# High and low part of each weight tile, 32 bytes apart modulo 64, under the 256-column passes of a two-layer encoder

## The chip, the cores and the metric

The kernel runs on one core of a Trainium2 chip, with no communication. The metric is the device time of one execution in microseconds (us). A profiled execution gives the time of every instruction on TensorE (PE, and PEld for its weight loads), VectorE (DVE), ScalarE (ACT), GpSimd (POOL) and SyncE (SP), and of the transfers.

## The reference

Two layers over 512 positions of 1024 channels, float32. Each layer has a half-step FFN, a mixer of three branches and a second half-step FFN, all behind an RMSNorm and a shift, scale and gate worked out from `c`:

```python
def swiglu(h, w_gate, w_up, w_down):
    return (jax.nn.silu(h @ w_gate) * (h @ w_up)) @ w_down
...
    for l in range(DEPTH):
        mod = (c_act @ w_ada[l] + b_ada[l]).reshape(B, N_MOD, D_MODEL)
        h = modulate(rms_norm(x, norm_gain[l, 0]), mod[:, 0], mod[:, 1])
        x = x + 0.5 * mod[:, 2][:, None, :] * swiglu(h, ffn_w_gate[l, 0], ffn_w_up[l, 0], ffn_w_down[l, 0])
        h = modulate(rms_norm(x, norm_gain[l, 1]), mod[:, 3], mod[:, 4])
        x = x + mod[:, 5][:, None, :] * hybrid_mixer(h, w_in[l], ...)
        h = modulate(rms_norm(x, norm_gain[l, 2]), mod[:, 6], mod[:, 7])
        x = x + 0.5 * mod[:, 8][:, None, :] * swiglu(h, ffn_w_gate[l, 1], ffn_w_up[l, 1], ffn_w_down[l, 1])
```

An FFN has 2816 hidden channels. The mixer (attention in chunks, trailing averages, attention with forget gates, their gated sum and an output map) has no part in the change but for its weight tiles' slots.

## The kernel before, in words

**Precision.** Every float32 operand is split into a high part, rounded to float32r, and the low remainder. ScalarE casts the high part (`nc.scalar.copy`), VectorE subtracts (`lo = raw - hi`). A product is three matmul passes, high·high, high·low, low·high, in that order: `triple` (lines 119 to 121) or, in the seven-product scheme, `add_product` (lines 128 to 130). In the order of the weight operand that is high, high, low, then the next 128 channels' high, high, low. A pass streams 512 columns of the moving operand, or 256.

**The FFN.** Hidden tiles of 128 channels are made in three parts of 6, 8 and 8. Some are made directly, with 512-column passes (`Ffn.unit`): all six of the first part in the opening FFN, the first four in the other three FFNs. The rest come in pairs from `seven`, which makes a product of a 2x2 block matrix with seven block products instead of eight. It loads two weight tiles, forms the sums S1 to S4 on VectorE, splits everything, and runs seven block products of four `add_product` steps each, all of 256 columns: A11·B11, A12·B21, S2·T2, S1·T1, S3·T3, S4·B22, A22·T4. `seven` is called for the gate and then for the up weights of a pair, by turns. The right-hand blocks T1 to T4 and B lie in `b`, `hhi` and `hlo`. The down projection runs in `k_outer`, weights outermost, 512 columns a pass. The last half of an FFN's down projection, and of the mixer's output map, is split into two halves of 256 columns (`before_last` given); there `prefetch_weights` also fetches the next stage's first weight tiles.

**Tiles.** `st(shape, dtype, tag, bufs)` takes a slot of a tag. High parts of weights have the tag `whi`, low parts `wlo`, three slots each of 4096 bytes a partition; in `seven`, A11/A12 and A22 are there, and the split sums S1/S2 and S3/S4 are in two tiles of tag `ptb` (two slots of 8192 bytes), high half first. Prefetched weights (`spare`) lie in `ptb` or `b`. `raw` receives the transfers, issued on SyncE's queue. Tags are laid out in order of first use and each slot's size is rounded up to 32 bytes. `whi`, `wlo`, `v2` and the tags ahead of them start on multiples of 64 bytes; `nt_v4` has 16 bytes, so `raw`, `t1`, `t2` and `ptb`, which follow it, start at 32 past a multiple of 64.

**Order.** The tile framework sets the order of instructions on each engine from the order of the program and its priorities, and semaphores where tiles are shared. Work on the side (the modulation's dot products on VectorE, norms) is spread by `later` and `poll`, which count passes by `pe[0]`.

Of the kernel before, what the change touches and what calls it, by code (L numbers as in the profile page):

```python
# [15 lines left out]
F32 = mybir.dt.float32  # L16
F32R = mybir.dt.float32r
# [5 lines left out]
P = 128  # L23
T = 512
D = 1024
KD = D // P
# [3 lines left out]
H = 8  # L30
# [10 lines left out]
def encoder_kernel(tc, xT, c, w_ada, b_ada, gains, w_gate, w_up, w_down, w_qkv, w_f, w_ubg,  # L41
# [18 lines left out]
    def nm(s):  # L60
        uid[0] += 1
        return f"{s}_{uid[0]}"

    def st(shape, dt, tag, bufs):
        return sb.tile(shape, dt, tag=tag, bufs=bufs, name=nm(tag))

    def acc(shape=(P, T)):
        return ps.tile(list(shape), F32, tag="acc", bufs=4, name=nm("acc"))

    def mmt(shape=(P, T)):  # L70
        return ps.tile(list(shape), F32, tag="mm", bufs=4, name=nm("mm"))

    def blk(tag, dt=F32R):
        bufs = {"xv": 4, "v2": 4, "b": NB}[tag]
        return st([P, 2, T], dt, tag, bufs)
# [65 lines left out]
    nc.scalar.dma_start(crow, c)  # L141
    nc.scalar.activation(crow, crow, AF.Silu)
    x_blocks, squares, crows = [], [], []
    for b in range(4):
        xb = blk("xv", F32)
        nc.sync.dma_start(xb, xT[:, 2 * b:2 * b + 2, :])
        x_blocks.append(xb)
        sq = st([P, 2, T], F32, "wlo" if b else "whi", 3)
        for a in range(2):
            nc.scalar.activation(sq[:, a, :], xb[:, a, :], AF.Square)  # L150
        squares.append(sq)
        if b < 2:
            pc = mmt()
            mm(pc, ones[0:1, :], crow[:, b * T:(b + 1) * T], start=True, stop=True)
            crows.append(pc)
# [117 lines left out]
                mod_credit[0] -= 1.0  # L273
                mod_pop()

    def wchunk(src, shape, side=True, spare=None, lo_eng=None):
        lo_eng = lo_eng or nc.vector
        side_work(side)
        raw = st([P] + list(shape), F32, *(("b", NB) if spare else ("raw", NRAW)))
        last["dma"] = nc.sync.dma_start(raw, src).ins  # L280
        if spare == "ptb":
            both = st([P, 2] + list(shape), F32R, "ptb", 2)
            hi, lo = both[:, 0], both[:, 1]
        elif spare == "b":
            hi = st([P] + list(shape), F32R, "b", NB)
            lo = st([P] + list(shape), F32R, "b", NB)
        else:
            hi = st([P] + list(shape), F32R, "whi", 3)
            lo = st([P] + list(shape), F32R, "wlo", 3)
        with behind("scalar"):  # L290
            nc.scalar.copy(hi, raw)  # L291
        with behind("vector"):
            lo_eng.tensor_tensor(lo, raw, hi.bitcast(F32), op=ALU.subtract)  # L293
        return hi, lo
# [102 lines left out]
    def split_to(hi, lo, src):  # L397
        nc.scalar.copy(hi, src)  # L398
        nc.vector.tensor_tensor(lo, src, hi.bitcast(F32), op=ALU.subtract)  # L399


    def k_outer(chunk_src, nch, lhs_rhs, before_last=None):

        if before_last is None:
            parts, nheld = [(None, slice(0, T), [acc() for _ in range(4)])], 2
        else:
            parts = [(hs, slice(hs * HALF, (hs + 1) * HALF), [b((P, HALF)) for _ in range(4)])
                     for hs, b in enumerate((mmt, acc))]  # L410
            nheld = 3

        def go(part, j, chunks):
            _, cols, accs = part
            for c, hi, lo in chunks:
                for kk in range(2):
                    a, b, x, y = lhs_rhs(hi[:, kk, :], lo[:, kk, :], 2 * c + kk, j)
                    triple(accs[j], a, b, x[:, cols], y[:, cols], start=(c == 0 and kk == 0),
                           stop=(c == nch - 1 and kk == 1))

        held = []
        for c in range(nch):
            if before_last is not None:
                if c == nch - 2:
                    quiet[0] = 8
                    before_last()
                quiet[0] = 8
            hi, lo = wchunk(chunk_src(c), (2, T))
            if c < nch - nheld:
                for part in parts:  # L430
                    for j in range(4):
                        go(part, j, [(c, hi, lo)])
            else:
                held.append((c, hi, lo))
        if before_last is not None:
            quiet[0] = 5
        for part in parts:
            for j in range(4):
                go(part, j, held[:-2])
            for j in range(4):  # L440
                go(part, j, held[-2:])
                yield j, part[0], part[2][j]
# [23 lines left out]
    def minus(o, a, b):  # L466
        nc.vector.tensor_tensor(o, a, b, op=ALU.subtract)  # L467
# [51 lines left out]
            q0, cols = {"T1": (0, FIRST), "T3": (0, SECOND), "T4": (2, FIRST), "T2": (2, SECOND)}[name]  # L519
            return [tuple(part[:, k % 2, cols] for part in self.parts[q0 + k // 2]) for k in range(4)]  # L520

    def seven(srcs, blocks, bank):

        raws = []
        for src in srcs:
            side_work()
            raw = st([P, KD, P], F32, "raw", NRAW)
            last["dma"] = nc.sync.dma_start(raw, src).ins
            raws.append(raw)
        tens = lambda o, a, b, op: nc.vector.tensor_tensor(o, a, b, op=op)  # L530
        a11, a12, a21, a22 = raws[0][:, :4], raws[0][:, 4:], raws[1][:, :4], raws[1][:, 4:]
        ah, al = st([P, KD, P], F32R, "whi", 3), st([P, KD, P], F32R, "wlo", 3)
        split_to(ah, al, raws[0])
        bh, bl = st([P, 4, P], F32R, "whi", 3), st([P, 4, P], F32R, "wlo", 3)
        split_to(bh, bl, a22)
        s12, s34 = st([P, 2, 4, P], F32, "v2", 4), st([P, 2, 4, P], F32, "v2", 4)
        tens(s12[:, 0], a21, a22, ALU.add)
        minus(s34[:, 0], a11, a21)
        minus(s12[:, 1], s12[:, 0], a11)
        minus(s34[:, 1], a12, s12[:, 1])  # L540
        pair12, pair34 = st([P, 2, 2, 4, P], F32R, "ptb", 2), st([P, 2, 2, 4, P], F32R, "ptb", 2)
        split_to(pair12[:, 0], pair12[:, 1], s12)
        split_to(pair34[:, 0], pair34[:, 1], s34)
        lefts = {"A11": [(ah[:, k], al[:, k]) for k in range(4)],
                 "A12": [(ah[:, 4 + k], al[:, 4 + k]) for k in range(4)],
                 "A22": [(bh[:, k], bl[:, k]) for k in range(4)]}
        for name, pair, i in (("S1", pair12, 0), ("S2", pair12, 1), ("S3", pair34, 0), ("S4", pair34, 1)):
            lefts[name] = [(pair[:, 0, i, k], pair[:, 1, i, k]) for k in range(4)]
        x, y, w = bank((P, HALF)), bank((P, HALF)), bank((P, HALF))
        c = st([P, 4, HALF], F32, "v2", 4)  # L550
        go = lambda o, left, right, start: add_product(o, lefts[left], blocks.operand(right), start)
        go(x, "A11", "B11", True)
        nc.scalar.copy(c[:, 0], x)
        go(y, "A12", "B21", True)
        tens(c[:, 0], y, c[:, 0], ALU.add)
        go(x, "S2", "T2", False)
        nc.scalar.copy(c[:, 1], x)
        go(w, "S1", "T1", True)
        nc.scalar.copy(c[:, 2], w)
        go(x, "S3", "T3", False)  # L560
        nc.scalar.copy(c[:, 3], x)
        go(w, "S4", "B22", False)
        tens(c[:, 1], w, c[:, 1], ALU.add)
        tens(c[:, 3], c[:, 2], c[:, 3], ALU.add)
        go(x, "A22", "T4", False)
        return [[c[:, 0:2].rearrange("p a t -> p (a t)")], [x, c[:, 3]]]
# [10 lines left out]
    class Ffn:  # L577
# [9 lines left out]
            self.norm = Norm(self.l, self.ms, xtag)  # L587

        def prefetch_weights(self):
            self.pre = [self.gate_up(0, 0, spare="ptb"), self.gate_up(1, 0, spare="ptb"), self.gate_up(0, 1, spare="b")]  # L590

        def unit(self, o, w, cols=slice(0, T), ks=range(KD)):
            for k in ks:
# [16 lines left out]
        def run(self, nxt):  # L610
            l, s, ms = self.l, self.s, self.ms
            in_ffn[0] = True
            mod_tag[0] = "v2"
            parts = ((0, 6), (6, 8), (14, 8))
            for part, (f0, nf) in enumerate(parts):
                acts = []
                n = 0
                if part == 0 and self.norm is None:
                    acts = self.start()
                    n = 3  # L620
                    blocks = Blocks()
                elif part == 0:
# [17 lines left out]
                    n = 2  # L640
                    blocks = Blocks(self.norm.xa, modc[:, l, 3 * ms])
# [16 lines left out]
                    blocks.finish()  # L658
                while n < nf:
                    both = [apply(p, AF.Silu)  # L660
                            for p in seven([w_gate[l, s, f0 + n + i] for i in range(2)], blocks, acc)]
                    ups = seven([w_up[l, s, f0 + n + i] for i in range(2)], blocks, mmt)
                    for i, sg in enumerate(both):
                        acts.append(self.act(n + i, None, ups[i], sg))
                    n += 2
# [235 lines left out]


    def forget(l):
        raw = st([P, KD, H], F32, "wf", 1)
        nc.sync.dma_start(raw, w_f[l])
        f2 = st([P, KD, 40], F32R, "ssum", 1)
        nc.gpsimd.memset(f2.bitcast(F32), 0.0)
# [10 lines left out]
        a = t2(T)[:H, :]  # L918
# [9 lines left out]
        for i in range(NT):  # L928
            n = (i + 1) * P
# [383 lines left out]
```

## Time and profile before

| | |
|---|---|
| median of 3 runs | 2387.72 us (2385.93 to 2392.21) |
| the profiled execution | 2390.61 us, its span 2388.7 us |
| TensorE busy | 2352.5 us, 98% of the span, 14322 matmuls |
| VectorE busy | 1766.9 us, 74% |
| ScalarE busy | 1219.5 us, 51% |
| transfers | 320.95 MB, mean 134 GB/s |

A matmul's record in the profile runs from its start to its modelled end and overlaps the next one's; how long a pass holds the engine is the spacing of two starts. Line numbers are those of the kernel before. A group's row gives the engine, the operation, the tiles written and read (`acc<-b,whi`: into `acc`, moving operand `b`, weights `whi`), shape and count.

### The profile page before, as it was taken

What the parts mean: (1) busy time and instruction counts of PE and PEld (TensorE: products, weight loads), DVE (VectorE), ACT (ScalarE), POOL (GpSimd) and SP (SyncE); (2) the same over time, 40 slices, a digit from 0 to 9 for tenths busy, and PEclk for the clock granted to TensorE, in tenths of its full rate; (3) what the DMA queues carried; (4) which work ended last, traced back from release to release, by engine and by line L of the source; (5) the groups of instructions that cost most, each with busy time, mean ns of one, the idle gap of its engine ahead of it and who ended that gap; (6) DMA issues with size and microseconds to landing.
All of it is one profiled execution on the core that took longest, in us unless ns stands there. A gap on an engine that the chain in (4) does not pass through costs nothing.

```text
span 2388.7 us, 37374 instructions
## 1 busy us (share of the span) xinstructions
PE 2352.5 (98%) x14322; PEld 2093.0 (88%) x14322; DVE 1766.9 (74%) x3147; ACT 1219.5 (51%) x2129; POOL 314.8 (13%) x401
## 2 busy tenths in 40 slices
PE   7999999999999999999999999999999999999999
PEld 5898998778888898989999989888788888999898
DVE  8887866787685577878687878677876855878583
ACT  5353555786632353535553536466865324636262
POOL 3000011144412200000100000112443122000000
PEclk9999999999999999999999999999999999999999
DMA  8535342323355524353415353523233654143323
GB/s 278 192 106 185 99 167 80 94 76 112 113 198 207 185 72 159 115 183 101 150 63 177 99 184 107 185 72 115 73 114 110 220 197 173 62 141 107 98 101 103
DMA packets 116438, 320.95 MB, mean 134 GB/s; under 512 B 11138, under 2 KB 13314, under 8 KB 116260
## 3 DMA queue, kind: packets, MB, share of 16 engines
q1 hardware_dynamic: 115106, 314.38, 39.7%
q0 software_dynamic: 1152, 4.19, 0.4%
q8 instruction: 112, 1.84, 0.3%
q14 instruction: 66, 0.54, 0.1%
q10 hardware_dynamic: 2, 0.00, 0.0%
HBM read 312.16 MB, written 6.38 MB: 133 GB/s over the span
## 4 chain that ended last, share of the span: by engine, by line
PE 84%; DVE 7%; ACT 5%; issue 2%; DMA 2%; SPq 0%; ACTq 0%; DVEq 0%
PE acc L119 15%; PE acc L120 15%; PE acc L121 15%; PE acc L128 4%; PE acc L129 4%; PE mm L128 4%; PE mm L129 4%; PE acc L130 4%; PE mm L130 4%; PE mm L119 3%; PE mm L121 3%; PE mm L120 3%; DVE v L206 1%; ACT b L863 1%; PE mm L1001 1%
## 5 line engine op out<-in xcount | busy, mean ns | idle before, releaser
L291 ACT CAST whi<-raw 128x1024 fp32r<-128x1024 f32 (+1 forms) x255 | 264.8, 1043 | 376.5 <-PE acc L120 246.0
L293 DVE TENSOR_TENSOR wlo<-raw,whi 128x1024 fp32r<-128x1024 f32 x247 | 303.8, 1233 | 154.2 <-ACT whi L291 153.0
L119 PE MATMUL acc<-b,whi 128*128 128x512 f32 (+1 forms) x960 | 360.6, 376 | 0.0
L120 PE MATMUL acc<-b,whi 128*128 128x512 f32 (+1 forms) x960 | 357.0, 372 | 0.0
L121 PE MATMUL acc<-b,wlo 128*128 128x512 f32 (+1 forms) x960 | 356.6, 371 | 0.0
L121 PEld LDWEIGHTS acc<-b,wlo 128*128 128x128 f32 x960 | 180.8, 188 | 31.7
L119 PEld LDWEIGHTS acc<-b,whi 128*128 128x128 f32 x960 | 180.8, 188 | 31.2
L120 PEld LDWEIGHTS acc<-b,whi 128*128 128x128 f32 x960 | 181.0, 189 | 29.6
L399 DVE TENSOR_TENSOR ptb<-v,ptb 128x1024 fp32r<-128x1024 f32 x140 | 171.2, 1224 | 36.9 <-ACT ptb L398 36.8
L398 ACT CAST ptb<-v 128x1024 fp32r<-128x1024 f32 x140 | 146.7, 1051 | 100.8 <-DVE v L467 52.7
L119 PE MATMUL acc<-hhi,whi 128*128 128x512 f32 x480 | 191.2, 400 | 3.3 <-ACT hhi L728 1.7
L120 PE MATMUL acc<-hlo,whi 128*128 128x512 f32 x480 | 187.9, 392 | 2.1 <-DVE hlo L731 2.1
L121 PE MATMUL acc<-hhi,wlo 128*128 128x512 f32 x480 | 187.6, 391 | 0.0
L398 ACT CAST whi<-raw 128x1024 fp32r<-128x1024 f32 (+1 forms) x140 | 116.7, 834 | 120.6 <-PE acc L120 55.2
L399 DVE TENSOR_TENSOR wlo<-raw,whi 128x1024 fp32r<-128x1024 f32 (+1 forms) x140 | 133.2, 951 | 8.2 <-ACT whi L398 6.8
L119 PE MATMUL acc<-whi,hhi 128*128 128x512 f32 x336 | 137.8, 411 | 0.9 <-DVE xv L399 0.9
L121 PE MATMUL acc<-whi,hlo 128*128 128x512 f32 x336 | 132.0, 393 | 0.0
L120 PE MATMUL acc<-wlo,hhi 128*128 128x512 f32 x336 | 131.7, 392 | 0.0
L206 DVE CUSTOM_DVE_ANT_0 v<-v,b,badac 128x1024 f32<-128x1024 f32 x87 | 115.7, 1339 | 12.3 <-DMA v<-in_w_ada_dram 12.2
L448 DVE SCALAR_TENSOR_TENSOR xv<-acc,modc,xv 128x512 f32<-128x512 f32 (+1 forms) x112 | 77.1, 691 | 56.3 <-PE acc L121 56.2
L129 PE MATMUL acc<-b,ptb 128*128 128x256 f32 x420 | 118.1, 281 | 0.0
L129 PE MATMUL mm<-b,ptb 128*128 128x256 f32 x420 | 118.1, 281 | 0.0
(313 smaller groups left out, 6662.2 us busy)
## 6 DMA issues: line engine op xcount, KB each, us to landing
raw<-in_w_down_dram SPq DMA_DIRECT2D x88, 512.0 KB, 4.4
v<-in_w_ada_dram SPq DMA_DIRECT2D x87, 512.0 KB, 4.9
raw<-in_w_up_dram SPq DMA_DIRECT2D x82, 512.0 KB, 3.6
raw<-in_w_gate_dram SPq DMA_DIRECT2D x79, 512.0 KB, 3.6
b<-in_w_ada_dram SPq DMA_DIRECT2D x57, 512.0 KB, 5.3
raw<-in_w_ubg_dram SPq DMA_DIRECT2D x56, 512.0 KB, 3.6
raw<-in_w_qkv_dram SPq DMA_DIRECT2D x42, 512.0 KB, 3.8
raw<-in_w_branch_dram SPq DMA_DIRECT2D x24, 512.0 KB, 3.7
```

The source lines that it names most:

```text
L119: mm(o, lh, rh, start=start, stop=False)
L120: mm(o, lh, rl, start=False, stop=False)
L121: mm(o, ll, rh, start=False, stop=stop)
L128: mm(o, lh, rh, start=start and k == 0, stop=False, skip_group_check=True)
L129: mm(o, lh, rl, start=False, stop=False, skip_group_check=True)
L130: mm(o, ll, rh, start=False, stop=k == 3, skip_group_check=True)
L206: dot = nc.vector.tensor_tensor_reduce(out=raw, in0=raw, in1=silc[0], scale=1.0, scalar=badac[:, l, j, d:d + 1], op0=ALU.mult, op1=ALU.add ...
L291: nc.scalar.copy(hi, raw)
L293: lo_eng.tensor_tensor(lo, raw, hi.bitcast(F32), op=ALU.subtract)
L398: nc.scalar.copy(hi, src)
L399: nc.vector.tensor_tensor(lo, src, hi.bitcast(F32), op=ALU.subtract)
L448: nc.vector.scalar_tensor_tensor(x, acc_j, gate, x, op0=ALU.mult, op1=ALU.add)
```

## The change

A new helper, `duo`, takes one slot for both parts of a tile: 4·512+16 words, the high part from the start and the low part from word 1024, each moved by a number of words that a table `PLACES` gives for the tag and the place. `whi` and `wlo` become one tag `w`, and `ptb` weights use `duo` too. For `w`, place 0 moves neither part; place 1 moves the high part 32 bytes and the low part 64; place 2 moves the low part 32 bytes. For `ptb`, place 0 moves both 32 bytes, place 1 the low part 32, place 2 the high part 32 and the low part 64. `seven` takes place 1 for the gate and place 2 for the up weights; the split `k_outer` takes place 1; the prefetched first gate and up tiles take 1 and 2; all else takes 0. The squares of the start lie in two `w` slots, and the forget weights' 256 bytes move from a tag of their own into `yl`.

```diff
+    PLACES = {("w", 0): (0, 0), ("w", 1): (8, 16), ("w", 2): (0, 8),
+              ("ptb", 0): (8, 8), ("ptb", 1): (0, 8), ("ptb", 2): (8, 16)}
+
+    def duo(shape, tag="w", place=0, raw=False):
+
+        t = st([P, 4 * T + 16], F32R, tag, {"w": 3, "ptb": 2}[tag])
+        n = int(np.prod(shape))
+        parts = []
+        for base, at in zip((0, 2 * T), PLACES[tag, place]):
+            v = t[:, base + at:base + at + n]
+            if len(shape) == 2:
+                v = v.rearrange("p (a b) -> p a b", a=shape[0])
+            elif len(shape) == 3:
+                v = v.rearrange("p (a b c) -> p a b c", a=shape[0], b=shape[1])
+            parts.append(v)
+        return parts
...
+    sq_parts = duo((2, T)) + duo((2, T))
...
-        sq = st([P, 2, T], F32, "wlo" if b else "whi", 3)
+        sq = sq_parts[b].bitcast(F32)
...
-    def wchunk(src, shape, side=True, spare=None, lo_eng=None):
+    def wchunk(src, shape, side=True, spare=None, lo_eng=None, place=0):
...
         if spare == "ptb":
-            both = st([P, 2] + list(shape), F32R, "ptb", 2)
-            hi, lo = both[:, 0], both[:, 1]
+            hi, lo = duo(shape, "ptb", place)
...
         else:
-            hi = st([P] + list(shape), F32R, "whi", 3)
-            lo = st([P] + list(shape), F32R, "wlo", 3)
+            hi, lo = duo(shape, "w", place)
...
-            hi, lo = wchunk(chunk_src(c), (2, T))
+            hi, lo = wchunk(chunk_src(c), (2, T), place=0 if before_last is None else 1)
...
-    def seven(srcs, blocks, bank):
+    def seven(srcs, blocks, bank, place):
...
-        ah, al = st([P, KD, P], F32R, "whi", 3), st([P, KD, P], F32R, "wlo", 3)
+        ah, al = duo((KD, P), "w", place)
         split_to(ah, al, raws[0])
-        bh, bl = st([P, 4, P], F32R, "whi", 3), st([P, 4, P], F32R, "wlo", 3)
+        bh, bl = duo((4, P), "w", place)
...
-        pair12, pair34 = st([P, 2, 2, 4, P], F32R, "ptb", 2), st([P, 2, 2, 4, P], F32R, "ptb", 2)
-        split_to(pair12[:, 0], pair12[:, 1], s12)
-        split_to(pair34[:, 0], pair34[:, 1], s34)
+        pair12, pair34 = duo((2, 4, P), "ptb", place), duo((2, 4, P), "ptb", place)
+        split_to(*pair12, s12)
+        split_to(*pair34, s34)
...
-            lefts[name] = [(pair[:, 0, i, k], pair[:, 1, i, k]) for k in range(4)]
+            lefts[name] = [(pair[0][:, i, k], pair[1][:, i, k]) for k in range(4)]
...
-            self.pre = [self.gate_up(0, 0, spare="ptb"), self.gate_up(1, 0, spare="ptb"), self.gate_up(0, 1, spare="b")]
+            self.pre = [self.gate_up(0, 0, spare="ptb", place=1), self.gate_up(1, 0, spare="ptb", place=2), self.gate_up(0, 1, spare="b")]
...
-                            for p in seven([w_gate[l, s, f0 + n + i] for i in range(2)], blocks, acc)]
-                    ups = seven([w_up[l, s, f0 + n + i] for i in range(2)], blocks, mmt)
+                            for p in seven([w_gate[l, s, f0 + n + i] for i in range(2)], blocks, acc, 1)]
+                    ups = seven([w_up[l, s, f0 + n + i] for i in range(2)], blocks, mmt, 2)
...
-        raw = st([P, KD, H], F32, "wf", 1)
+        raw = st([P, KD, H], F32, "yl", 1)
```

## The prediction

> **What bounds the kernel now.** I read the page first: the busy shares, the slices, the chain of waits.
>
> ```profile
> span 2388.7 us, 37374 instructions
> PE 2352.5 (98%) x14322; PEld 2093.0 (88%) x14322; DVE 1766.9 (74%) x3147; ACT 1219.5 (51%) x2129; POOL 314.8 (13%) x401
> ...
> PEclk9999999999999999999999999999999999999999
> ...
> PE 84%; DVE 7%; ACT 5%; issue 2%; DMA 2%; SPq 0%; ACTq 0%; DVEq 0%
> ```
>
> TensorE is busy for 98% of the span at the full granted clock, and the chain that ends last is 84% TensorE. Passes queue without gaps, so what a pass costs is not its record but its spacing: start to start with the next one. The windows view and the timeline give it. First, by stage: a stretch of eight pairs of seven-product calls (`seven`), and one split `k_outer`:
>
> ```profile
> core 0: us, PE busy (x) PEld busy (x) DVE busy (x) ACT busy (x) POOL busy (x), PEclk, DMA share, GB/s
> 954.89:1034.72 79.83, 79.83 (x673) 79.83 (x672) 70.10 (x105) 46.62 (x80) 0.00 (x0) 1.00 0.41 128
> 833.08:849.63 16.55, 16.55 (x139) 16.55 (x138) 10.67 (x12) 9.76 (x16) 4.86 (x5) 1.00 0.31 96
> ```
>
> (673 and 139 count one pass that reaches over an edge.) 79.83 us / 672 is 118.8 ns a pass in `seven`; 16.55 / 138 is 119.9 ns in the split `k_outer`. TensorE has no gap in either, and DVE's 70.10 us leave 12% of the first. All are 256-column passes; they still do not all cost the same. The tile view shows it (minimum/median/maximum of the record, ns):
>
> ```profile
> L128 PE MATMUL mm<-hhi,whi x280: 283/283/283, 134.9 to 2332.9; 128*128 128x256 f32 x140
> L129 PE MATMUL acc<-hlo,ptb x140: 277/280/285, 132.1 to 2328.7; 128*128 128x256 f32 x140
> L130 PE MATMUL acc<-hhi,ptb x140: 274/278/281, 132.3 to 2328.8; 128*128 128x256 f32 x140
> ```
>
> Same shape, same kind of moving operand; only the weight tile differs. With `whi` every record is 283, locked; with `ptb` it drifts from 277 to 285; and line 130 alone has records down to 274.
>
> The code says what differs. Slots are laid out by tag in order of first use. `hhi`, `hlo`, `b`, `xv`, `whi`, `wlo` and `v2` start on multiples of 64 bytes. Then comes the 16-byte `nt_v4` in a place of 32, and `raw`, `t1`, `t2` and `ptb` behind it start 32 past a multiple. So `whi`/`wlo` weights are in class 0, `ptb` weights in class 32, and the moving operands of these rows in class 0. Now the timeline over the two kinds of switch (start us, record us, instruction):
>
> ```profile
> 127.64 0.28 PE L130 MATMUL acc<-hhi,wlo 128*128 128x256 f32 x1
> 127.76 0.28 PE L128 MATMUL acc<-b,ptb 128*128 128x256 f32 x1
> 127.87 0.28 PE L129 MATMUL acc<-b,ptb 128*128 128x256 f32 x1
> 127.99 0.28 PE L130 MATMUL acc<-b,ptb 128*128 128x256 f32 x1
> ...
> 133.20 0.28 PE L129 MATMUL acc<-hlo,ptb 128*128 128x256 f32 x1
> 133.32 0.27 PE L130 MATMUL acc<-hhi,ptb 128*128 128x256 f32 x1
> 133.43 0.28 PE L128 MATMUL acc<-b,whi 128*128 128x256 f32 x1
> 133.55 0.28 PE L129 MATMUL acc<-b,whi 128*128 128x256 f32 x1
> 133.66 0.28 PE L130 MATMUL acc<-b,wlo 128*128 128x256 f32 x1
> ...
> 134.86 0.28 PE L128 MATMUL mm<-hhi,whi 128*128 128x256 f32 x1
> ...
> 137.74 0.28 PE L128 MATMUL mm<-b,ptb 128*128 128x256 f32 x1
> ```
>
> 134.86 to 137.74 is 24 class-0 passes in 2.88 us: 120 ns each, locked. That goes with the record of 283, so record less 163 is about the spacing. 127.76 to 133.43 is 48 class-32 passes in 5.67 us: 118.1 ns. The switch 32 to 0 (pass at 133.32, record 0.27, the 274 above) has about 111 to 113 ns, and the three passes from it take 0.34 us against 0.36 for three locked ones. The switch 0 to 32 (127.64) has 0.12 and then 0.11: three passes in 0.35. Other calls repeat it at the same places:
>
> ```profile
> 143.30 0.27 PE L130 MATMUL mm<-hhi,ptb 128*128 128x256 f32 x1
> 143.41 0.28 PE L128 MATMUL mm<-b,whi 128*128 128x256 f32 x1
> 143.53 0.28 PE L129 MATMUL mm<-b,whi 128*128 128x256 f32 x1
> 143.64 0.28 PE L130 MATMUL mm<-b,wlo 128*128 128x256 f32 x1
> ...
> 153.28 0.27 PE L130 MATMUL acc<-hhi,ptb 128*128 128x256 f32 x1
> ...
> 153.62 0.28 PE L130 MATMUL acc<-b,wlo 128*128 128x256 f32 x1
> ```
>
> 0.34 us both times. Today such switches come twice in 84 passes. The change makes them come twice in three.
>
> **The change, part by part.**
>
> *1. High and low part in opposite classes, in `seven`.* A `w` slot has 4·512+16 words, 8256 bytes or 129·64, so all its slots start in class 0, and those of `ptb` stay in class 32. The places add 0, 32 or 64 bytes. Gate (place 1): high in class 32, low in class 0, in both tags. Up (place 2): high 0, low 32. Each group of three passes uses high, high, low, so it has one pair of equal weights and two switches. A gate group, from the rows: high to low (32 to 0) 113 ns, low to high (0 to 32) 118, and the equal pair behind a switch to 32, which began 127.76, 116 (0.11 to 0.12): 347 ns. An up group: 118, 113, and 117 for the equal pair behind a switch to 0: 348. The mean is 115.8 ns against 118.8 now. `Ffn.run` calls `seven` twice for each pair of hidden tiles: 1, 4 and 4 pairs in three FFNs, 4 and 4 in the opening one, so 3·18 + 16 = 70 calls of 7·4·3 = 84 passes: 5880. They lie on the path (no gap in that window): 5880 · 3.0 ns = 17.6 us less.
>
> No row shows such a mix in steady state, so I bound it: every pass at the shortest record, 274 (about 112.5 ns), saves 5880 · 6.3 ns = 37 us; every pass at the longest, 285 (about 122), costs 5880 · 3.2 = 19 us. I take the switch rows, because they are the same operation, repeated at three places with the same answer.
>
> *2. The split `k_outer`, place 1.* 4 FFNs and 2 output maps, 192 passes each, 1152: from 119.9 to the gate group's 115.7: 4.8 us less. Bounds as before: 8.5 less, 2.4 more.
>
> *3. The prefetched first gate and up tile in `ptb`.* 288 passes (3 FFNs · 2 tiles · 8 · 2 halves · 3). Gate and up alternate here from one k to the next, and opposite order puts low next to an equal high: one switch each way in six passes, not two. I take half the effect, about 1.5 ns: 0.4 us less.
>
> *4. The mixer's two prefetched tiles, default place, now class 0.* They are the moving operand of 96 passes:
>
> ```profile
> 384.65 0.39 PE L119 MATMUL acc<-ptb,hhi 128*128 128x512 f32 x1
> ...
> 385.82 0.39 PE L120 MATMUL acc<-ptb,hhi 128*128 128x512 f32 x1
> ...
> 1057.19 0.39 PE L119 MATMUL acc<-b,whi 128*128 128x512 f32 x1
> ...
> 1058.78 0.39 PE L120 MATMUL acc<-b,whi 128*128 128x512 f32 x1
> ```
>
> Five spacings in 1.17 us are 234 ns; seven in 1.59 are 227. 96 · 7 ns = 0.7 us less. All other 512-column weight tiles stay in class 0 (place 0) and keep 227.
>
> *5. One slot for both parts.* A high tile's slot now comes free with the low part's last pass, one pass (0.23 us) later. The group view has who feels it:
>
> ```profile
> L291 ACT CAST whi<-raw 128x1024 fp32r<-128x1024 f32 (+1 forms) x255 | 264.8, 1043 | 376.5 <-PE acc L120 246.0
> ```
>
> and the waits of TensorE (us in all, times, longest) have what it costs there:
>
> ```profile
> PE acc L119 <- ACT whi L291: 1.6, 2, 0.8
> PE mm L119 <- ACT whi L291: 1.5, 1, 1.5
> ```
>
> The cast waits for that slot often (246.0 us), with DVE's subtraction queued behind it, but TensorE waits for a cast only three times, 3.1 us in all: the other two slots cover it. I cost it at 0.5 us; uncovered at all of ScalarE's 88 such waits it would be 88 · 0.23 = 20 us, which the three waits exclude. The opening squares hold two of three slots until DVE's fold, long before the second weight tile's cast. The small forget weights move into `yl`, idle then; its one transfer on SP's queue waits for nothing.
>
> *Sum:* 17.6 + 4.8 + 0.4 + 0.7 − 0.5 = 23 us. The profiled execution took 2390.6 us (span 2388.7), 0.1% above the median of 2387.7, so the scale is the same: 2388 − 23 is 2365. I put 2366, as DVE, at 70.10 of 79.83 us, would come to 90% of that stage and may hold back a little. The bounds of parts 1 and 2 set the forecast's own range: 2352 (three quarters of the 45 us) to 2378.
>
> [...] The rows above have 283 throughout with one weight tile and 274 to 285 with another. [...]
>
> **The rivals.**
>
> *Paid back.* The short pass at a switch belongs to the state that the long drift before it left; the mix settles near the drifting 118 ns. For: the 12 passes 133.43 to 134.86 take 1.43 us, 119.2 each, so a switch is mostly gone after a few passes. Against: the gain itself is not taken back in them, 1.43 us against 1.44 for twelve locked. At 117.3 ns: 5880 · 1.5 + 1152 · 2.6 = 12 us, 2376; at 118, 2381.
>
> [...]
>
> *Slower: the mix catches at the long spacing.* Class 0 alone locks at 120; alternating classes could lock as well, and at a drift's longest records (285, about 122 ns) rather than its shortest. The place is `seven` and the split `k_outer`; it decides from a mean of 118.8 up; at 122 it costs 19 + 2 = 21 us: 2409; half of it 2398. For: a lock exists, and the drift holds such records. Against: each switch seen so far ran short, none long.
>
> **How the numbers follow.** Forecast 0.55; paid back 0.15; nothing 0.10; slower 0.20. The range reaches from the forecast's low end, 2352, over paid back and nothing to the mildest of slower, 2394. About 0.3% (7 us) is what a measurement of this kernel can tell from no change. Faster: 0.55 and most of paid back, 0.67. Same: the rest of it and nothing, 0.13. Slower: 0.20.
>
> **What would show it.** Right: the stretch of eight pairs of calls takes 77.5 to 78.5 us instead of 79.83, with TensorE still gapless; a 138-pass split takes 16.0; weight records in `seven` leave 283 for about 274 to 281; 512-column spacing stays 227. Paid back: records spread round 280 and the stretch takes 79. Slower: records of 285 as the median. Wrong in part 5: new idle time of TensorE behind casts.

## The result, and the profile after

The changed kernel took 2401.93 us (median of 4 runs, 2401.36 to 2403.82) against 2388.55 us for the kernel before (2385.93 to 2392.21): a ratio of 1.0056 with a 95% interval of 1.0039 to 1.0074, 0.56% slower. The forecast was 2366 us, with a range of 2352 to 2394: sign and range both failed.

The page of the changed kernel, its busy shares and clock:

```profile
span 2399.6 us, 37345 instructions
PE 2367.1 (99%) x14322; PEld 2088.5 (87%) x14322; DVE 1774.6 (74%) x3147; ACT 1217.5 (51%) x2129; POOL 303.2 (13%) x401
...
PEclk9999999999999999999999999999999999999999
```

As many matmuls as before, at the full granted clock, and TensorE is busy for 14.6 us longer (2352.5 before): passes got longer, nothing new is waited for. The windows view says which. For the changed kernel, in this order: the stretch of 672 passes of `seven` (eight calls of 84 passes, so four pairs of a gate and an up call, where the prediction speaks of eight pairs), the split `k_outer`, and a down projection of 192 passes of 512 columns:

```profile
core 0: us, PE busy (x) PEld busy (x) DVE busy (x) ACT busy (x) POOL busy (x), PEclk, DMA share, GB/s
961.29:1040.82 79.53, 79.53 (x673) 79.53 (x672) 69.83 (x106) 46.64 (x80) 0.00 (x0) 1.00 0.39 133
838.05:854.73 16.68, 16.58 (x139) 16.36 (x138) 10.89 (x12) 9.64 (x16) 4.85 (x5) 1.00 0.29 95
2226.97:2271.44 44.47, 44.47 (x194) 36.09 (x193) 20.55 (x25) 11.07 (x12) 0.00 (x0) 1.00 0.25 83
```

The same down projection in the kernel before:

```profile
2216.95:2260.50 43.55, 43.55 (x194) 36.05 (x193) 20.82 (x25) 11.08 (x12) 0.00 (x0) 1.00 0.29 85
```

`seven` gained almost nothing: 79.53 us against 79.83, 118.3 ns a pass against 118.8. The place that the prediction had left alone lost: 43.55 / 192 is 226.8 ns a pass, 44.47 / 192 is 231.6. TensorE has no gap in either. The tile view (minimum/median/maximum of the records, ns) shows the same; first the changed kernel, where lines 136 to 138 are `triple` and 145 to 147 `add_product`:

```profile
L136 PE MATMUL acc<-hhi,w x480: 387/393/796, 21.9 to 1998.8; 128*128 128x512 f32 x160
L145 PE MATMUL acc<-hhi,w x280: 277/280/288, 126.0 to 2333.6; 128*128 128x256 f32 x140
L146 PE MATMUL acc<-hlo,ptb x140: 277/281/288, 133.2 to 2339.4; 128*128 128x256 f32 x140
L147 PE MATMUL acc<-hhi,ptb x140: 277/280/288, 133.3 to 2339.5; 128*128 128x256 f32 x140
```

and the 512-column row of the kernel before:

```profile
L119 PE MATMUL acc<-hhi,whi x480: 387/389/795, 22.4 to 1990.1; 128*128 128x512 f32 x160
```

The 512-column median went from 389 to 393. In these rows of `seven` the records left 283, as forecast, but for 277 to 288 with a median of 280 or 281, not for the short ones.

Added up from start to start over the whole trace (sums over all passes, in us; no row of the page has them):

| passes | before | after | difference |
|---|---|---|---|
| 512 columns, `triple`, 5664 | 1318.7 us | 1337.9 us | +19.2 |
| 256 columns, `seven`, 5880 | 701.3 | 698.7 | −2.6 |
| 256 columns, `triple`, 1583 | 196.0 | 190.6 | −5.4 |
| sum | | | +11.2 |

The spans differ by 10.9 us. Of the 5.4 us, 3.6 are idle time, not pace (what spacings have above 130 ns went from 6.4 to 2.8 us). Below, a mean spacing "without waits" leaves out the spacings above 130 ns.

**Which 512-column passes.** The kernel's slots for `w` hold 4·512+16 words, 8256 bytes or 32·256 + 64. In the compiled program they start at 121856, 130112 and 138368: 0, 64 and 128 bytes past a multiple of 256. Before, the slots of 4096 bytes all started at 0. Four tiles of 24 passes in the down projection above (the second and third lie in the slot at 0, the first in that at 64, the last in that at 128):

```profile
2226.97:2232.59 5.62, 5.62 (x26) 4.50 (x25) 3.14 (x5) 2.06 (x3) 0.00 (x0) 1.00 0.25 84
2232.59:2238.07 5.48, 5.48 (x25) 4.50 (x24) 1.23 (x1) 1.05 (x1) 0.00 (x0) 1.00 0.30 102
2249.24:2254.72 5.48, 5.48 (x26) 4.51 (x24) 2.91 (x3) 1.05 (x1) 0.00 (x0) 1.00 0.46 139
2254.72:2260.31 5.59, 5.59 (x26) 4.53 (x24) 1.23 (x1) 1.05 (x1) 0.00 (x0) 1.00 0.46 147
```

234.2, 228.3, 228.3 and 232.9 ns a pass, one kernel, one stage, one code line. That gave the theory: **the slot's size moved the 512-column weights off a multiple of 256 bytes**. The rivals: the alternation inside `seven` itself costs the time; or the shared slot does, by coming free later.

### The profile page after: what moved, and what is told of

The parts are those of the page before. It is cut to its first block, busy times and chain, and to the rows that moved or that the text cites. A ratio compares the mean times of both kernels' runs of the same rounds, so it can differ in the third digit from the quotient of the medians.

```text
span 2399.6 us, 37345 instructions
## 1 busy us (share of the span) xinstructions
PE 2367.1 (99%) x14322; PEld 2088.5 (87%) x14322; DVE 1774.6 (74%) x3147; ACT 1217.5 (51%) x2129; POOL 303.2 (13%) x401
## 4 chain that ended last, share of the span: by engine, by line
PE 84%; DVE 7%; ACT 5%; issue 2%; DMA 1%; SPq 0%; DVEq 0%; ACTq 0%; POOL 0%; POOLq 0%
PE acc L136 15%; PE acc L138 15%; PE acc L137 15%; PE mm L147 4%; PE mm L146 4%; PE mm L145 4%; PE acc L145 4%; PE acc L146 4%; PE acc L147 4%; PE mm L136 3%; PE mm L138 3%; PE mm L137 3%; ACT b L879 1%; PE mm L1017 1%; DVE v L224 1%
## 5 line engine op out<-in xcount | busy, mean ns | idle before, releaser
L309 DVE TENSOR_TENSOR w<-raw,w 128x1024 fp32r<-128x1024 f32 x247 | 315.5, 1281 | 165.8 <-ACT w L307 165.5
L307 ACT CAST w<-raw 128x1024 fp32r<-128x1024 f32 (+1 forms) x255 | 263.8, 1039 | 283.8 <-PE acc L138 199.5
L136 PE MATMUL acc<-b,w 128*128 128x512 f32 (+1 forms) x960 | 363.4, 379 | 0.0
L138 PE MATMUL acc<-b,w 128*128 128x512 f32 (+1 forms) x960 | 360.3, 375 | 0.0
L137 PE MATMUL acc<-b,w 128*128 128x512 f32 (+1 forms) x960 | 360.1, 375 | 0.0
L138 PEld LDWEIGHTS acc<-b,w 128*128 128x128 f32 x960 | 180.4, 188 | 34.9
L136 PEld LDWEIGHTS acc<-b,w 128*128 128x128 f32 x960 | 180.7, 188 | 34.5
L137 PEld LDWEIGHTS acc<-b,w 128*128 128x128 f32 x960 | 180.6, 188 | 33.4
L136 PE MATMUL acc<-hhi,w 128*128 128x512 f32 x480 | 192.7, 403 | 3.3 <-ACT hhi L744 1.7
L137 PE MATMUL acc<-hlo,w 128*128 128x512 f32 x480 | 189.3, 394 | 1.7 <-DVE hlo L747 1.7
L138 PE MATMUL acc<-hhi,w 128*128 128x512 f32 x480 | 189.2, 395 | 0.0
L414 ACT CAST w<-raw 128x1024 fp32r<-128x1024 f32 (+1 forms) x140 | 116.5, 832 | 126.8 <-PE acc L138 58.2
L415 DVE TENSOR_TENSOR w<-raw,w 128x1024 fp32r<-128x1024 f32 (+1 forms) x140 | 133.1, 950 | 13.4 <-ACT w L414 13.3
L136 PE MATMUL acc<-w,hhi 128*128 128x512 f32 x336 | 138.2, 412 | 0.6 <-DVE xv L415 0.6
L138 PE MATMUL acc<-w,hlo 128*128 128x512 f32 x336 | 132.4, 394 | 0.0
L137 PE MATMUL acc<-w,hhi 128*128 128x512 f32 x336 | 132.0, 393 | 0.0
L224 DVE CUSTOM_DVE_ANT_0 v<-v,b,badac 128x1024 f32<-128x1024 f32 x87 | 115.6, 1339 | 10.6 <-DMA v<-in_w_ada_dram 10.6
L147 PE MATMUL mm<-b,ptb 128*128 128x256 f32 x420 | 118.5, 282 | 0.0
L146 PE MATMUL mm<-b,ptb 128*128 128x256 f32 x420 | 118.1, 281 | 0.0
```

The lines of the kernel that those rows point to most:

```text
L136: mm(o, lh, rh, start=start, stop=False)
L137: mm(o, lh, rl, start=False, stop=False)
L138: mm(o, ll, rh, start=False, stop=stop)
L146: mm(o, lh, rl, start=False, stop=False, skip_group_check=True)
L147: mm(o, ll, rh, start=False, stop=k == 3, skip_group_check=True)
L224: dot = nc.vector.tensor_tensor_reduce(out=raw, in0=raw, in1=silc[0], scale=1.0, scalar=badac[:, l, j, d:d + 1], op0=ALU.mult, op1=ALU.add ...
```

## The experiments

A ratio in this section is to the kernel before, run on the same chip, with its 95% interval.

**1. The pace by address, measured alone (map_offsets).** A stretch is 72 passes in groups of high, high, low, with the two weight tiles moved by a number of words.

```python
def stretch(n, hi, lo, groups=24):
    for g in range(groups):
        k = g % 4
        a = w[:, hi + k * P:hi + (k + 1) * P]
        b = w[:, 2 * T + lo + k * P:2 * T + lo + (k + 1) * P]
        x, y = m[:, 0, k, :n], m[:, 1, k, :n]
        nc.tensor.matmul(acc, a, x, start=g == 0, stop=False)
        nc.tensor.matmul(acc, a, y, start=False, stop=False)
        nc.tensor.matmul(acc, b, x, start=False, stop=g == groups - 1)
```

> A kernel of its own: the encoder is left out (the output is the input x), and what runs is 60 stretches of 72 passes each, in the order high, high, low over four weight blocks of 512 bytes, with weights in one tile whose base is a multiple of 512 bytes. Per stretch the high part is moved by a and the low part by b words of 4 bytes; first 30 pairs (a, b) under 256 columns, then the same 30 under 512. Slot theory (what matters under 512 columns is the weight address modulo more than 64 bytes): 512-column spacing is 227 ns at (0,0) and (128,128) and about 230 to 233 ns at (16,16) and (32,32), which are all the same modulo 64 bytes; 256-column spacing is 120 at (0,0) and about 118 for nearly all others, alternating or not. Class theory of the prediction (only the class modulo 64 bytes matters, and a switch of 32 bytes shortens): 512-column spacing is 227 at all of (0,0), (16,16), (32,32), (128,128); 256-column spacing is 116 or less at (8,0), (0,8), (8,16) and (16,8) and 118 to 120 where both parts are equal.

The windows of eight stretches: 256 columns with (high, low) moved by (0, 0), (32, 32), (64, 64) and (32, 0) bytes; then 512 columns with (0, 0), (32, 32), (64, 64) and (256, 256):

```profile
34.67:43.30 8.63, 8.63 (x74) 8.63 (x72) 0.00 (x0) 0.00 (x0) 0.00 (x0) 1.00 0.01 2
51.83:60.35 8.52, 8.52 (x75) 8.52 (x74) 0.00 (x0) 0.00 (x0) 0.00 (x0) 1.00 0.00 0
68.82:76.99 8.17, 8.17 (x75) 8.17 (x74) 0.00 (x0) 0.00 (x0) 0.00 (x0) 1.00 0.00 0
137.20:145.69 8.49, 8.49 (x75) 8.49 (x74) 0.00 (x0) 0.00 (x0) 0.00 (x0) 1.00 0.01 2
291.38:307.73 16.35, 16.35 (x75) 13.52 (x74) 0.00 (x0) 0.00 (x0) 0.00 (x0) 1.00 0.00 1
324.05:340.84 16.79, 16.79 (x74) 13.53 (x72) 0.00 (x0) 0.00 (x0) 0.00 (x0) 1.00 0.00 1
357.64:374.43 16.79, 16.79 (x74) 13.53 (x72) 0.00 (x0) 0.00 (x0) 0.00 (x0) 1.00 0.00 0
441.39:457.72 16.33, 16.33 (x73) 13.51 (x72) 0.00 (x0) 0.00 (x0) 0.00 (x0) 1.00 0.00 1
```

The length of each window over 72 is the pace, the run-in included. Without the run-in (mean of the last 48 spacings, the step to the next stretch among them, ns):

| (high, low), bytes | 256 columns | 512 columns |
|---|---|---|
| (0, 0) | 119.96 | 226.67 |
| (32, 32) | 118.33 | 233.27 |
| (64, 64) | 113.42 | 233.21 |
| (128, 128) | 118.75 | 233.35 |
| (192, 192) | 117.77 | 228.88 |
| (256, 256) | 120.00 | 226.79 |
| (32, 0) | 117.83 | 231.92 |
| (0, 32) | 118.33 | 233.33 |
| (32, 64) | 118.67 | 231.17 |
| (64, 32) | 120.02 | 235.48 |

With 512 columns the short pace is at 0 and comes back at 256 bytes, not at 64: by this map a pass costs 6.5 ns more at 64 and 6.7 more at 128. Of the kernel's 4488 512-column passes with weights in `w`, 1422 lie at 0, 1686 at 64 and 1380 at 128: 1686 · 6.5 + 1380 · 6.7 is 20.2 us. In the two traces these 4488 passes differ by 18.7 of the 19.2 us, so the loss is theirs. But the parts do not fit as well as the total: 9.3 us at 64, 7.1 at 128, and 2.2 at 0, where the map has nothing. With 256 columns, parts 32 bytes apart give 117.8 to 120.0 in this table, not 115.8: against the 118.8 that `seven` had before, that is between 1.0 ns less and 1.2 more, not 3.0 less. In this map only equal parts at 64 bytes are short, 113.42, which neither theory had expected.

**2 and 3. No alternation, with the change's slot and with a tight one (zero_places, zero_tight).**

```diff
-    PLACES = {("w", 0): (0, 0), ("w", 1): (8, 16), ("w", 2): (0, 8), ...
+    PLACES = {(tag, place): (0, 0) for tag in ("w", "ptb") for place in range(3)}
 # zero_tight has this too:
-        t = st([P, 4 * T + 16], F32R, tag, {"w": 3, "ptb": 2}[tag])
+        t = st([P, 4 * T], F32R, tag, {"w": 3, "ptb": 2}[tag])
```

> The changed kernel with every place set to (0, 0): one slot of 8256 bytes for both parts as in the change, but high and low part in the same class modulo 64 everywhere. Slot theory: the 512-column passes stay at about 231 ns, 19 us above before in all, and the 256-column passes leave the lock as well because two of three slots are off multiples of 512; 2398 to 2404 us, as slow as the change. Alternation theory (the opposite classes under 256 columns cost the time): back at 2388. Shared-slot theory (one slot for both parts makes a cast wait for the low part's last pass): 2401, with new idle time of TensorE behind casts.

> As zero_places, but the slot has 8192 bytes, so every slot of w is on a multiple of 512 bytes again; both parts still share a slot. Slot theory: 512-column spacing back at 227 and the time at 2388 (2385 to 2391). Shared-slot theory: still about 2401.

zero_places: 2402.83 us, ratio 1.0062 (1.0049 to 1.0075), as slow as the change. zero_tight: 2389.34 us, ratio 1.0003 (0.9994 to 1.0012). The stretch of `seven` and the down projection in zero_places,

```profile
961.57:1040.86 79.29, 79.29 (x673) 79.16 (x672) 69.84 (x106) 46.61 (x80) 0.00 (x0) 1.00 0.42 134
2226.60:2271.03 44.43, 44.43 (x195) 36.10 (x193) 20.56 (x25) 11.07 (x12) 0.00 (x0) 1.00 0.25 83
```

and in zero_tight:

```profile
955.48:1035.31 79.83, 79.83 (x673) 79.83 (x672) 70.33 (x106) 46.85 (x80) 0.00 (x0) 1.00 0.41 133
2214.21:2257.76 43.55, 43.55 (x195) 36.08 (x193) 20.52 (x25) 11.07 (x12) 0.00 (x0) 1.00 0.28 85
```

With no alternation at all the down projection is at 44.43 us; 64 bytes less in the slot bring it to 43.55. Both rivals fall: the loss is there without the alternation (1.0062), and one slot for both parts cost nothing that can be told (1.0003) with slots of 8192 bytes, a multiple of 256.

**4. The change with slots that keep their class (aligned_slots).** The room comes from `dynamic_dma_scratch_size`, here and in the three kernels of runs 7 to 9.

```diff
-        t = st([P, 4 * T + 16], F32R, tag, {"w": 3, "ptb": 2}[tag])
+        t = st([P, 4 * T + 128], F32R, tag, {"w": 3, "ptb": 2}[tag])
-    nc = _bacc.Bacc("TRN2", target_bir_lowering=False, num_devices=1)
+    nc = _bacc.Bacc("TRN2", target_bir_lowering=False, num_devices=1, dynamic_dma_scratch_size=8192)
```

> The change with all its places, but slots of 8704 bytes (17 times 512) instead of 8256; the room comes from GpSimd's descriptor memory, which is set to 8192 bytes instead of 16384. Slot theory: 512-column spacing back at 227 for place 0, 256-column spacing about 118.3 in seven and in the split k_outer, so some 5 to 8 us below before: 2380 to 2384. Alternation theory: 2395 to 2401, as the change. Shared-slot theory: about 2401.

2387.53 us, ratio 0.9996 (0.9987 to 1.0005). The same two stretches:

```profile
956.30:1037.17 80.87, 80.25 (x674) 79.85 (x673) 69.91 (x105) 46.62 (x80) 0.00 (x0) 1.00 0.42 132
2215.24:2258.79 43.55, 43.55 (x195) 36.07 (x193) 20.53 (x25) 11.09 (x12) 0.00 (x0) 1.00 0.27 85
```

The down projection is back at 43.55 us and the loss is gone. What is left is the alternation as meant, and it brings nothing that can be told from zero_tight: over all of `seven` its mean without waits is 118.6 ns against 118.8 before, 1.0 us over 5880 passes. By offsets it runs as mapped, 118.3 at (0, 32) and 118.7 at (32, 64); the third pair that it has, (64, 96), runs at 118.7. (The first stretch has 0.62 us of idle time in this profile.) The 5 to 8 us that I still expected of it did not come.

**5. Gate and up in the same order (same_order).**

```diff
-    ... ("w", 2): (0, 8), ... ("ptb", 2): (8, 16)
+    ... ("w", 2): (8, 16), ... ("ptb", 2): (0, 8)
```

> The change with gate and up in the same order (place 2 as place 1: high part in class 32, low part in class 0 for both; slots of 8256 bytes as in the change). Lock theory: nothing hangs on the order, the slots off multiples of 256 bytes stay and with them the 512-column passes at 231 ns: 2399 to 2405. A theory that the opposite order itself costs: 2390 or less.

2403.01 us, ratio 1.0056 (1.0043 to 1.0070): the opposite order of gate and up neither costs nor brings anything that can be told.

**6. A second map, with the moving operand moved too (map_more).** The same stretches with a third number for the moving tile (`x, y = m[:, 0, k, mo:mo + n], m[:, 1, k, mo:mo + n]`).

> A second map; the encoder is left out (the output is the input x). 59 stretches of 72 passes: one of 512 columns at (0,0), then 29 settings (a, b, c) under 256 columns and the same under 512: high part moved by a, low part by b, moving operand by c words of 4 bytes, all bases on multiples of 256 bytes. Lock theory (the address modulo 256 relative to the moving operand's counts): 256-column spacing is 113.4 at (16,16,0), (80,80,0), (16,80,0), (32,32,16) and (24,24,8); it is 120 at (16,16,16) and (16,16,... moved alike). If the weight address counts by itself, (16,16,16) gives 113.4 and (32,32,16) about 118.8 as (32,32,0) did.

Five stretches of 256 columns, (high, low, moving) in bytes: (64, 64, 0), (64, 192, 0), (64, 64, 64), (0, 0, 64) and (0, 0, 192):

```profile
59.80:67.96 8.16, 8.16 (x75) 8.16 (x74) 0.00 (x0) 0.00 (x0) 0.00 (x0) 1.00 0.01 2
152.37:160.53 8.16, 8.16 (x75) 8.16 (x73) 0.00 (x0) 0.00 (x0) 0.00 (x0) 1.00 0.01 2
219.58:228.22 8.64, 8.64 (x75) 8.64 (x73) 0.00 (x0) 0.00 (x0) 0.00 (x0) 1.00 0.00 0
228.22:236.70 8.48, 8.48 (x75) 8.48 (x73) 0.00 (x0) 0.00 (x0) 0.00 (x0) 1.00 0.01 2
236.70:244.87 8.17, 8.17 (x75) 8.17 (x73) 0.00 (x0) 0.00 (x0) 0.00 (x0) 1.00 0.01 2
```

Moved together by 64 bytes, the pace is that of nothing moved (119.98 with 256 columns, 226.67 with 512). A moving tile at 192 under weights at 0 gives 113.42 and 233.27, like weights at 64; one at 64 gives 117.8 and 228.9, like weights at 192. So in the maps it is the distance of weights and moving operand, modulo 256, that counts. Two points do not fit exactly. Weights at 96 over a moving operand at 32 gave 117.79 where I expected 113.4; that is the pace of a second rhythm that lock64 shows below. And in the first map (384, 384) gave 120.06 and 232.56 where (128, 128) gave 118.75 and 233.35. Weights moved by 8 bytes gave 115.58, and parts at 64 and 192 held 113.33.

**7 to 9. The weights of `seven`, the split `k_outer` and the prefetched `ptb` tiles at the best distances (lock64, off8, lock64_192).** Slots of 8448 bytes, 33·256, place 0 on a multiple of 256 in both tags, and both other places alike, in words:

```diff
+        t = st([P, 4 * T + 64], F32R, tag, {"w": 3, "ptb": 2}[tag])
+    # lock64:      ("w", 1 and 2): (16, 16), ("ptb", 1 and 2): (8, 8),   ("ptb", 0): (56, 56)
+    # off8:        ("w", 1 and 2): (2, 2),   ("ptb", 1 and 2): (58, 58), ("ptb", 0): (56, 56)
+    # lock64_192:  ("w", 1 and 2): (16, 48), ("ptb", 1 and 2): (8, 40),  ("ptb", 0): (56, 56)
```

> A version meant to beat both. Slots of 8448 bytes (33 times 256; the room again from GpSimd's descriptor memory at 8192 bytes), and no opposite classes: under 256 columns both parts of every weight tile lie 64 bytes past a multiple of 256 (places 1 and 2: both parts moved 64 bytes in w, 32 in ptb, whose slots start 32 past one), under 512 columns both on a multiple of 256 (place 0 of ptb moves both by 224). Lock theory from the map of offsets (spacing is set by the weight address modulo 256 relative to the moving operand's, 113.4 ns at 64 under 256 columns, 226.7 at 0 under 512): seven falls from 118.8 to 113.4 ns (5880 passes, 32 us), the split k_outer from 119.9 to 113.4 (1152, 7 us), the prefetched tiles by 1 us; 2346 to 2352, and the stretch of eight pairs of calls takes about 76.3 us instead of 79.83, unless DVE (70.1 us of work there) holds back some of it. Rival, drift theory (in the encoder, with products changing accumulators and tiles, the short lock is lost and any place off 0 gives about 118): 2380 to 2388.

> As lock64, but both parts 8 bytes past a multiple of 256 under 256 columns, where the second map had 115.6 ns with a rhythm of 115, 115, 117. If that holds in seven whatever state it is entered from: 118.8 to 115.6 on 5880 passes and 119.9 to 115.6 on 1152, 24 us less: 2363 to 2369. If it too has a slower state of about 118: 2380 to 2386.

> As lock64, but under 256 columns the high part lies 64 and the low part 192 bytes past a multiple of 256 (both 64 past a multiple of 128, but 128 bytes apart). The second map had 113.3 ns for this pair, entered from the 113 ns state, and in lock64 the passes of seven were in a state of 113 ns for one part and in one of 117.8 for the rest. If the apart pair has no state of 117.8 to fall into, seven comes to 113.4 to 114.5 but for the waits behind ScalarE's copies that lock64 began to show: 2360 to 2372. If the slower state is there too: 2378 to 2384, as lock64.

| | us | ratio (95%) | mean pass in `seven`, without waits |
|---|---|---|---|
| lock64 | 2380.78 | 0.9966 (0.9953 to 0.9978) | 116.4 ns |
| off8 | 2376.88 | 0.9949 (0.9937 to 0.9962) | 115.6 ns |
| lock64_192 | 2371.20 | 0.9929 (0.9916 to 0.9943) | 113.5 ns |

off8 runs at its mapped pace, but its time misses the 2363 to 2369 that I expected: what spacings of its `seven` have above 130 ns is 13.0 us, against 2.6 before. lock64 does not run at its mapped pace, and its time is that of the rival: its passes keep one of two rhythms, 113/113/114 or one about 117.8, and it stayed in the second more than half the time (3994 spacings of 117 to 119 against 1810 of 113 and 114), though its stretch in the maps held the first. Two of its up calls, 84 passes each, the same addresses modulo 256, no pause in either:

```profile
980.37:990.26 9.89, 9.89 (x87) 9.89 (x85) 7.95 (x12) 5.94 (x11) 0.00 (x0) 1.00 0.35 99
1000.51:1010.03 9.52, 9.52 (x86) 9.52 (x85) 7.81 (x12) 5.99 (x11) 0.00 (x0) 1.00 0.36 111
```

The rhythm changes 15 times in this trace: nine changes stand within five passes behind a spacing above 130 ns, five where `seven` resumes after other work, one at neither. lock64_192 keeps 113 or 114 in 5612 of 5880. Why 64 and 192 hold the rhythm here and 64 twice does not, is open.

lock64_192 beats the kernel before by 17.6 us (2388.82 on its chip), and with it the changed kernel. Its passes alone would give more: over the 7463 256-column passes of `seven` and `triple` the mean without waits falls from 118.95 to 113.76 ns, 39 us, but the sum of their spacings only from 897.4 to 876.2, 21 us. Nearly half of the gain turns into waiting. In the last stretch of 672 passes of `seven` all of it does. That stretch before and in lock64_192:

```profile
2260.50:2340.34 79.84, 79.84 (x674) 79.83 (x673) 66.95 (x101) 46.65 (x81) 0.00 (x0) 1.00 0.34 113
2241.92:2321.75 79.83, 77.58 (x673) 76.71 (x672) 66.77 (x101) 45.85 (x80) 0.00 (x0) 1.00 0.36 113
```

and the waits of TensorE over the whole execution (us in all, times, longest):

```profile
PE acc L145 <- ACT v L577: 13.1, 24, 0.7
PE mm L145 <- ACT v L577: 1.4, 2, 1.1
```

the first of them in the changed kernel:

```profile
PE acc L145 <- ACT v L577: 1.2, 3, 0.5
```

The stretch has 2.25 us without TensorE where it had none. Line 577 is ScalarE's copy of a running sum of products (`x` in `seven`) before the last product adds to it. One such wait in the timeline, ScalarE first, then TensorE:

```profile
2258.77 1.05 ACT L414 CAST ptb<-v 128x1024 fp32r<-128x1024 f32 x1 [1.29 <-DVE v L483]
2259.72 0.36 ACT L577 COPY v<-mm 128x256 f32<-128x256 f32 x1
...
2260.14 0.39 PE L145 MATMUL mm<-b,w 128*128 128x256 f32 x1 [0.36 <-ACT v L577]
```

The copy stands in ScalarE's queue behind the cast of the sums for `ptb`, and that cast had waited 1.29 us for VectorE's subtraction (line 483). TensorE has one product, 12 passes, to cover it: 1.42 us at 118 ns a pass, 1.36 at 113.5. So the shorter passes meet the chain from VectorE over ScalarE's cast to the copy, 26 times, 14.5 us; in all 26 the copy ran directly behind such a cast. Counted from start to start these 26 pauses hold 18.8 us above the pace, and the pass behind each, at some 220 ns, 2.8 us more; the net loss is smaller, as other waits shrank. A version with the copies ahead of the casts was not tried.

## Why the prediction failed, point by point

**What bounds the kernel** held: at a constant clock the time moved by what passes of TensorE cost, but for 3.6 us of idle time that went.

**Part 1, the size.** 115.8 ns in `seven` was forecast; 118.3 came, and 118.6 with clean slots. The switch rows (113, 118, 116) are in the trace as read, but they are not the passes of a group of three. The step that failed is the price of a switch: its 113 ns stands behind the last of 48 passes of one class (133.32), while in a group a switch stands behind one or two. A row for that was shown beside it: the second `ptb` pass behind a switch, from 127.87 to 127.99, takes 0.12. In the trace before, the first two spacings behind a switch to 32 are 115.8 and 121.6 ns (means over the 68 without a pause), behind a switch to 0 they are 116.7 and 118.3. A gate group made of these takes 354.1 ns, 118.0 a pass, and an up group 350.8, 116.9: a mean of 117.5, some 8 us of gain in place of 17.6. The map's steady (32, 0) and (0, 32) are 117.8 and 118.3. This is the rival "paid back", which I gave 0.15, at its upper end of 118. I had taken three agreeing repeats as evidence for the steady state; they were three observations of the same passage from one long run to another.

**Part 2** failed in the same way: the 138-pass split took 16.68 us (16.58 busy) where 16.0 were forecast and 16.55 came before; the mean without waits over all 256-column `triple` passes is 118.4 against 119.5. **Part 3** is inside that number and cannot be told apart.

**Part 4, the sign.** "All other 512-column weight tiles stay in class 0 (place 0) and keep 227" is the sentence that cost the sign: the sum has nothing for these passes, and they took 18.7 us more. It rests on "its slots all start in class 0", true modulo 64 and beside the point: modulo 256, two of three slots moved. Part of the evidence was in hand, in the same paragraph: its own rows have 512-column passes at 234 and at 227 ns whose operands lie at different addresses, and the two classes were all that the kernel before happened to contain, as all `whi` and `wlo` weights sat at 0 and all `ptb` at 32 modulo 256. A modulus was inferred from two points. Of the gain that I took for the mixer's 96 passes about half came: 233.5 to 230.3 ns a pass without waits, not 227. The changed size put half of these tiles at 64 under weights at 0, where the second map has 228.9.

**Part 5** was right: in the changed kernel TensorE waits for a cast twice, 1.6 us in all,

```profile
PE acc L136 <- ACT w L307: 1.6, 2, 0.8
```

against 3.1 us before, and zero_tight shows the shared slot at 1.0003.

**The rivals.** The time, 2401.9, lies within "slower" (2398 to 2409), but not by its mechanism: `seven` did not catch at 122 ns; it gained 2.6 us. No rival had the slot's size. The line under "what would show it" that did catch it is "512-column spacing stays 227". In the forecast's own range three quarters of the 45 us would be 2354, not 2352, and the upper end, 2378, has no working; nothing hung on either.

## What to carry to other kernels

A change of a buffer's size changes the addresses of the slots behind it: compare the addresses of all weight tiles in the compiled program before and after, modulo 256 at least (in the map 512 columns took 226.67 ns at 0, 233.21 at 64 and 226.79 at 256), and those of the tiles that the edit does not mean to touch first. The short spacing at a switch, 113 ns behind 48 passes of one class, was that of one switch after a long steady run; with switches in every group the first map's pairs at 0, 32 and 64 have 117.8 to 120.0. So measure the steady pattern by itself, in a stretch of some 70 passes. When passes become shorter, look for what each of them had covered: here nearly half of a gain of 39 us went into waits, most of them for one copy behind a cast.

## What the runs showed of the hardware

In the maps, with no work on VectorE, ScalarE and GpSimd in the windows shown, the spacing of float32r passes depends on the distance of the weight tile from the moving operand modulo 256 bytes (points at one distance agree to within 1.3 ns, but for one that has the second rhythm): 226.67 ns at 0 to 235.5 at the worst pair mapped with 512 columns; 113.3 (64, or 64 and 192) to 124.4 (high part at 160, low at 128) with 256. With 512 columns 16 bytes to either side of 0 keep the short pace (226.85 at 16, 226.67 at 240), 8 bytes past 0 do not (230.6). The best distance for the one length is not that of the other: of those mapped, 0 has the shortest pace with 512 columns (226.67, as 240 has) and one of the slow ones with 256 (119.96). At the same distance a pace can have two rhythms (113.3 and about 117.8); in lock64 14 of 15 changes stand at a pause or where `seven` resumes. The mechanism behind both is not shown here.
